# First net of a two-layer model: fourth and fifth chunk by seven block products, the half-wide chunk between them

## The chip, the core and the metric

The kernel runs on one core of a Trainium2 chip. The metric is the device time of one execution in microseconds (us), median of several runs. The five engines that matter are PE (TensorE, matrix products), DVE (VectorE), ACT (ScalarE), POOL (GpSimd) and SP (SyncE, which issues most DMA transfers). Each engine works its own queue of instructions in order; semaphores tie the queues together.

## The reference

Two layers, a sequence of 256 tokens, width 1024, everything in float32. A layer has two feed-forward nets (`ffn1`, `ffn2`) with a mixer and a cross attention between them. A net is

```python
def swiglu(x, w_gate, w_up, w_down):
    return (jax.nn.silu(x @ w_gate) * (x @ w_up)) @ w_down

h = layer_norm(ALPHA * h + 0.5 * swiglu(h, ffn1_gate[l], ffn1_up[l], ffn1_down[l]), ln_g[l, 0], ln_b[l, 0])
```

with `w_gate` and `w_up` of 1024 x 2816 and `w_down` of 2816 x 1024. The inner width of 2816 is five chunks of 512 columns and one of 256. The change touches only the first net of the first layer.

## The kernel before, in words

**Numbers in two parts.** A float32 matrix is split into a high part `hi` (rounded to the PE's own format, by ACT) and a low part `lo = x - hi` (by DVE); this is `split`, lines 61 and 62. A product is then three matmuls, hi x hi, hi x lo and lo x hi (`mm_rows`, through `product` at L105). Every weight that comes from HBM passes this way: a `raw` tile of 128 x 1024 lands by DMA (SP), ACT writes `whi`, DVE writes `wlo`, PE reads both. There are 6 `raw` buffers and 8 each of `whi` and `wlo`, so the splits can run at most 8 tiles ahead of PE.

**A chunk of a net** (`ffn`, L400 on) computes gate and up for 512 inner columns and all 256 tokens, then silu(gate) * up, then turns the result (`turn`: four DMAs `dealt`, DVE block transposes `square`, and a split into `ah` and `al`) so that it can be the stationary side of the down product. The down product of a chunk is two slabs, `both(c, 0)` and `both(c, 1)`, of 24 matmuls each, two weight tiles per slab, summed in four PSUM tiles `dn`. The slabs of a chunk are issued behind the gate and up products of later chunks, so that the turn is hidden. Three slabs, `end`, are held back to the layer norm (`finish`): there they are worked output half by output half (`tail`), 18 matmuls for each of the four `dn` tiles, so that the norm of the first tokens can begin while the rest is still being summed.

**Three ways to make a chunk.**
- `hidden`: 48 matmuls for gate and 48 for up; 8 weight tiles, each read for 12 matmuls; on DVE 8 splits and four multiplications `gated` (L440).
- `last_hidden`: the chunk of 256 columns, 64 matmuls (half of them of 256 columns), 4 weight tiles.
- `by_seven`: gate and up side by side are one 1024 x 1024 matrix, x is 256 x 1024; cut into 2 x 2 blocks, their product takes seven block products (Strassen's scheme in Winograd's form) in place of eight. A block product (`run`) is 12 matmuls. The sums of blocks of x (`bx`) are made once per net. The sums of weight blocks are made by DVE for each chunk: `parts_of` with `plus` adds two tiles of 128 x 1024 (L597), four times two additions. Each of the seven products then needs two tiles split, 14 in all, and each tile is read for 6 matmuls. The results are combined on DVE from PSUM by seven `put` (L619); `left` does the last three, then silu and two multiplications (L649), then `turn`. Four raw blocks are held at once: in `spare0` and `spare1`, in `lng` and `lnb` (the buffers of the norm's parameters, filled later by `ln_params`, L296 and L297), in two `raw`, and in `spare2` and one `raw`.

**The order of the first net before** (`early` is not None there): first, hidden(1), hidden(2), hidden(3), seven(4), half(5). From the third chunk on, chunk c is followed by slab 1 of chunk c-2 and slab 0 of chunk c-1. Beside hidden(1) and hidden(2), DVE also makes `bx`, turns the second input `mem` (`turned`, in `spare0` and `spare1`) and computes small parameters (L268 to L288, whose rows lie in `spare2`). The other three nets use `sevens = (2, 4)` and are not touched.

**Who orders what.** The instructions of an engine are put in a fixed order when the program is built; loads are issued ahead as buffers come free, and SP issues them strictly in order, so a load that waits for its buffer holds back all loads behind it.

Of the kernel before, what the change touches and what calls it, by code (L numbers as in the profile page):

```python
# [28 lines left out]
CHUNK = 512  # L29
# [17 lines left out]
def model(ctx: ExitStack, tc: tile.TileContext, t: dict, out: bass.AP):  # L47
# [12 lines left out]
    def split(hi, lo, src):  # L60
        nc.scalar.copy(hi, src)  # L61
        lows.append(nc.vector.tensor_tensor(lo, src, hi.bitcast(F32), op=ALU.subtract))  # L62

    def load(src, k0, nk, c0, ncol, fine=False):


        hi, lo, todo = [], [], []
        step = 2048 // ncol
        for a in range(k0, k0 + nk, step):
            half = step // 2  # L70
            raw = [
                wp.tile([P, 1024], F32, tag="raw", name="raw", bufs=6).rearrange("p (k c) -> p k c", c=ncol)
                for _ in range(2)
            ]
            part = 1 if fine else half
            for b in range(0, step, part):
                loads.append(nc.sync.dma_start(
                    raw[b // half][:, b % half : b % half + part, :],
                    src[(a + b) * P : (a + b + part) * P, c0 : c0 + ncol].rearrange("(k p) c -> p k c", p=P),
                ))  # L80
            for s in range(2):
                h = wp.tile([P, 1024], F32R, tag="whi", name="whi", bufs=8)
                w = wp.tile([P, 1024], F32R, tag="wlo", name="wlo", bufs=8)
                h = h.rearrange("p (k c) -> p k c", c=ncol)
                w = w.rearrange("p (k c) -> p k c", c=ncol)
                r = raw[s]
                if fine:
                    todo += [(h[:, b, :], w[:, b, :], r[:, b, :]) for b in range(half)]
                else:
                    split(h, w, r)  # L90
                hi.append(h)
                lo.append(w)
        return Weights(hi, lo, half, todo)
# [20 lines left out]
    def mm_cols(w, cols, x):  # L114
        o = acc()
        for k in range(NK - 1):
            product(o, w.at(k, cols)[0], x[:, k], k == 0, False)
        for k in range(NK):
            product(o[:, 0, :], w.at(k, cols)[1], x[:, k, 0, :], False, False)
        product(o, w.at(NK - 1, cols)[0], x[:, NK - 1], False, True)  # L120
        return sums(o)

    def add(dst, o):
        dst = dst if len(dst.shape) == 3 else halves(dst)
        nc.scalar.copy(dst, o[:, 1])
        nc.vector.tensor_tensor(dst, o[:, 0], dst, op=ALU.add)
# [273 lines left out]
    def ffn(l, name, n, pend=None, last=False, early=None):  # L400
        gate, up, down = (t[f"{name}_{x}"][l] for x in ("gate", "up", "down"))
        with tc.tile_pool(name="ffn", bufs=2, reuse_waits="tile") as fp:
            acts = []

            def act_tiles():
                ah = fp.tile([P, 4, SEQ], F32R, tag="ah", name="ah", bufs=3)
                al = fp.tile([P, 4, SEQ], F32R, tag="al", name="al", bufs=3)
                return ah, al
# [5 lines left out]
            def all_products(w):  # L414
                o = [acc((P, CHUNK)) for _ in range(NT)]
                for a in range(0, NK, 2):
                    for i in range(NT):
                        for k in range(a, a + 2):
                            products(o[i], w, i, k)
                return o  # L420

            def activations():
                return fp.tile([P, NT, CHUNK], F32, tag="sg", name="sg", bufs=1)
# [10 lines left out]
            def activate(s, i, og):  # L434
                for v, o in by_two(s[:, i, :], og):
                    nc.scalar.activation(v, o, AF.Silu)

            def gated(s, i, ou):
                for v, o in by_two(s[:, i, :], ou):
                    nc.vector.tensor_tensor(v, o, v, op=ALU.mult)  # L440
# [5 lines left out]
            def turn(s):  # L446
                ah, al = act_tiles()
                x = fp.tile([P, 4, NT, P], F32, tag="dealt", name="dealt", bufs=1)
                for a in range(4):
                    nc.sync.dma_start(x[a * 32 : a * 32 + 32], s[:, :, a * P : (a + 1) * P])  # L450
                for i in range(NT):
                    d = fp.tile([P, 4, P], F32, tag="up", name="square")
                    nc.vector.transpose(
                        d.rearrange("p k (b r) -> p b k r", b=4), x[:, :, i, :].rearrange("p b (k j) -> p b k j", k=4)
                    )
                    split(ah[:, :, tok(i)], al[:, :, tok(i)], d)
                return ah, al
# [80 lines left out]
            def hidden(c0, between=lambda: None):  # L538
                s = activations()
                o = all_products(load(gate, 0, NK, c0, CHUNK))  # L540
                for i in range(NT):
                    activate(s, i, o[i])
                between()
                o = all_products(load(up, 0, NK, c0, CHUNK))
                for i in range(NT):
                    gated(s, i, o[i])
                return turn(s)
# [106 lines left out]
            def last_hidden(c0):  # L654

                ah, al = act_tiles()
                s = activations()[:, 0, :].rearrange("p (j c) -> p j c", j=2)
                r = fp.tile([P, 2, SEQ], F32, tag="up", name="up")
                for m, o in ((gate, s), (up, r)):
                    w = load(m, 0, NK, c0, 2 * P)  # L660
                    for j in range(2):
                        add(o[:, j, :], mm_cols(w, slice(j * P, (j + 1) * P), xT))
                    if m is gate:
                        nc.scalar.activation(s, s, AF.Silu)
                nc.vector.tensor_tensor(s, r, s, op=ALU.mult)
                for j in range(2):
                    split(
                        *(x[:, j, :].rearrange("p (i b r) -> p i b r", i=2, b=4) for x in (ah, al)),
                        s[:, j, :].rearrange("p (i r b) -> p i b r", i=2, b=4),
                    )  # L670
                return ah, al

            def slab(c, u):
                w = load(down, c * 4 + 2 * u, 2, 0, DM)
                ah, al = acts[c]
                return w, ah[:, 2 * u : 2 * u + 2, :], al[:, 2 * u : 2 * u + 2, :]


            sevens = (2, 4) if early is None else (4,)
            bx = []  # L680

            if early is None:
# [5 lines left out]
            chunks = [(c, min(CHUNK, DFF - c)) for c in range(0, DFF, CHUNK)]  # L688
# [7 lines left out]
            def both(c, u):  # L696
                a = slab(c, u)
                for i in range(NT):
                    for k in range(2):
                        for m in range(2):  # L700
                            apart = last and i == m == k == u == 1 and c == 3
                            rows_of(a, i, k, m, c == u == k == 0, apart)
# [6 lines left out]
                    else:  # L709
                        bx.extend(blocks_of_x())  # L710

            for c, (c0, ncol) in enumerate(chunks):
                if not c:
                    acts.append(first())
                    ys = [[acc((P, 512), "dn") for _ in range(2)] for _ in range(NT)]
                elif c in sevens:
                    left = by_seven(c0, bx)
                else:
                    if c in (1, 2) and early is not None:
                        acts.append(hidden(c0, aside))  # L720
                    else:
                        acts.append(hidden(c0) if ncol == CHUNK else last_hidden(c0))
                if c == 1 and early is None:
                    bx.extend(blocks_of_x())
                if c == max(sevens) + 1:
                    gb = ln_params(l, n)
                if c == 1 and early is not None:

                    with tc.issue_after(loads[-1].ins):
                        rest = early(fp)  # L730
                if c == 2 and early is not None:
                    with tc.issue_after(lows[-1].ins):
                        rest[0]()
                if c > 0:
                    if c > 1:
                        both(c - 2, 1)
                    if c in sevens:
                        acts.append(left())
                    if c < len(chunks) - 1:
                        both(c - 1, 0)  # L740
            end = [slab(4, 0), slab(4, 1), slab(5, 0)]

            def tail(i, m, cols, alone, between):
                for u, a in enumerate(end):
# [476 lines left out]
```

## Time and profile before

| | |
|---|---|
| time, median of 3 runs (lowest to highest) | 1070.83 us (1070.54 to 1071.65) |
| span of the profiled execution | 1068.8 us |
| median less span | 2.0 us |
| ACT busy | 642.4 us (60%) |
| POOL busy | 66.4 us (6%) |
| HBM read | 216.15 MB |

The profile has busy time by engine, the chain of work that ended last, groups of instructions by line with their mean duration and the idle time ahead of them, and a timeline. Durations of neighbours overlap: an instruction of an engine starts a little before the one ahead of it is reported done, so the cost of one more instruction in a row is the distance between starts, not its duration. Matmuls overlap more strongly: one lasts 380 ns, but they start about 216 ns apart.

### The profile page before, as it was taken

The page shows a single profiled execution, that of the slowest core. Times are in us where ns is not written, and L with a number is a line of the kernel's source. Part 1 is how long each engine was busy: PE and PEld are TensorE (multiplying, and loading weights), DVE is VectorE, ACT ScalarE, POOL GpSimd, SP SyncE. Part 2 cuts the span into 40 slices and gives each one's busy share as a digit, 9 for nine tenths or more (in the row PEclk, how much of TensorE's full clock was granted, in tenths as well). Part 3 has the DMA queues.
Part 4 walks back from the last instruction along what each step waited for, and adds up shares of the span by engine and source line. Part 5 has one row for each costly group of instructions (what it writes and reads, how often), then busy time and mean ns, then how long its engine had stood idle before and what let it go on. Part 6 is the DMA issues. An engine that isn't in the chain of part 4 may idle for free.

```text
span 1068.8 us, 16312 instructions
## 1 busy us (share of the span) xinstructions
PE 1059.3 (99%) x5966; PEld 937.7 (88%) x5966; DVE 946.3 (89%) x1318; ACT 642.4 (60%) x916; POOL 66.4 (6%) x114
## 2 busy tenths in 40 slices
PE   9999999999999999999999999999999999999997
PEld 7888888889899888888888888888898998888886
DVE  6977997998988799999799999788989787999996
ACT  7555664666557565656575557566764665656660
POOL 9700001000000000000000000010000000000000
PEclk9999999999999999999999999999999999999999
DMA  9997484755574575848675865856536665759461
GB/s 362 262 307 256 129 288 165 249 176 174 170 278 167 178 252 194 290 167 218 238 272 184 256 254 183 290 179 216 196 126 213 241 227 181 257 156 334 134 223 40
DMA packets 130895, 231.90 MB, mean 217 GB/s; under 512 B 9408, under 2 KB 48608, under 8 KB 130816
## 3 DMA queue, kind: packets, MB, share of 16 engines
q1 hardware_dynamic: 129024, 228.49, 64.8%
q0 software_dynamic: 1216, 1.20, 0.5%
q8 instruction: 47, 0.77, 0.3%
q10 hardware_dynamic: 576, 1.18, 0.3%
q14 instruction: 32, 0.26, 0.1%
HBM read 216.15 MB, written 1.05 MB: 203 GB/s over the span
## 4 chain that ended last, share of the span: by engine, by line
PE 99%; DMA 0%; DVE 0%; issue 0%; DVEq 0%
PE acc L105 65%; PE dn L105 31%; PE acc L172 1%; PE dn L923 1%; PE dn L982 0%; DMA h<-in_x_dram 0%; PE acc L491 0%; PE dn L981 0%; PE dn L971 0%; PE acc L1047 0%; PE dn L888 0%; DVE h L358 0%; DVE h L353 0%; PE dn L472 0%; DVE st L338 0%
## 5 line engine op out<-in xcount | busy, mean ns | idle before, releaser
L61 ACT CAST whi<-raw 128x1024 fp32r<-128x1024 f32 (+1 forms) x438 | 442.9, 1042 | 197.5 <-DVE raw L597 54.9
L62 DVE TENSOR_TENSOR wlo<-raw,whi 128x1024 fp32r<-128x1024 f32 (+1 forms) x438 | 515.7, 1209 | 32.6 <-ACT whi L61 29.0
L105 PE MATMUL acc<-whi,xT 128*128 128x512 f32 x1032 | 312.9, 380 | 0.0
L105 PEld LDWEIGHTS acc<-whi,xT 128*128 128x128 f32 x1032 | 195.1, 189 | 27.5
L105 PE MATMUL acc<-wlo,xT 128*128 128x512 f32 x516 | 195.6, 379 | 0.0
L105 PE MATMUL acc<-xT,whi 128*128 128x512 f32 x576 | 142.3, 383 | 0.2
L105 PE MATMUL dn<-whi,ah 128*128 128x512 f32 x346 | 131.5, 380 | 0.0
L105 PE MATMUL dn<-wlo,ah 128*128 128x512 f32 x346 | 131.2, 379 | 0.0
L105 PE MATMUL dn<-whi,al 128*128 128x512 f32 x346 | 131.2, 379 | 0.0
L105 PEld LDWEIGHTS acc<-xT,whi 128*128 128x128 f32 x576 | 104.0, 190 | 12.5 <-ACT whi L61 0.7
L105 PEld LDWEIGHTS acc<-wlo,xT 128*128 128x128 f32 x516 | 97.5, 189 | 13.8
L105 PE MATMUL dn<-whi,xT 128*128 128x512 f32 x288 | 87.9, 381 | 0.0
L105 PEld LDWEIGHTS acc<-xT,wlo 128*128 128x128 f32 x576 | 75.5, 191 | 3.9
L105 PE MATMUL acc<-xT,wlo 128*128 128x256 f32 x576 | 75.9, 275 | 0.0
L105 PEld LDWEIGHTS dn<-whi,al 128*128 128x128 f32 x346 | 65.4, 189 | 9.2
L105 PEld LDWEIGHTS dn<-wlo,ah 128*128 128x128 f32 x346 | 65.4, 189 | 9.2
L105 PEld LDWEIGHTS dn<-whi,ah 128*128 128x128 f32 x346 | 65.4, 189 | 9.1
L350 POOL TENSOR_TENSOR rs<-rs,nhalf 128x1 f32<-128x1 f32 x16 | 14.9, 930 | 833.6 <-DVE rs L346 598.1
L597 DVE TENSOR_TENSOR raw<-raw 128x1024 f32<-128x1024 f32 x56 | 66.2, 1217 | 0.4
L105 PEld LDWEIGHTS dn<-whi,xT 128*128 128x128 f32 x288 | 54.4, 189 | 7.7 <-DVE xT L62 0.3
L105 PE MATMUL dn<-wlo,xT 128*128 128x512 f32 x144 | 54.6, 379 | 0.0
L332 DVE SCALAR_TENSOR_TENSOR h<-h,dn 128x512 f32<-128x512 f32 x31 | 21.2, 683 | 32.9 <-PE dn L105 32.9
(234 smaller groups left out, 1277.5 us busy)
## 6 DMA issues: line engine op xcount, KB each, us to landing
raw<-in_ffn_up_dram SPq DMA_DIRECT2D x88, 512.0 KB, 5.3
raw<-in_ffn_down_dram SPq DMA_DIRECT2D x88, 512.0 KB, 6.6
raw<-in_ffn_gate_dram SPq DMA_DIRECT2D x84, 512.0 KB, 5.1
raw<-in_w_in_dram SPq DMA_DIRECT2D x48, 512.0 KB, 4.7
dealt<-sg SPq DMA_DIRECT2D x80, 128.0 KB, 4.7
raw<-in_ca_k_dram SPq DMA_DIRECT2D x16, 512.0 KB, 4.9
raw<-in_w_out_dram SPq DMA_DIRECT2D x16, 512.0 KB, 4.5
raw<-in_ca_v_dram SPq DMA_DIRECT2D x16, 512.0 KB, 5.3
```

What stands on the lines that cost most here:

```text
L61: nc.scalar.copy(hi, src)
L62: lows.append(nc.vector.tensor_tensor(lo, src, hi.bitcast(F32), op=ALU.subtract))
L105: nc.tensor.matmul(o, w, x, start=start, stop=stop)
L172: nc.tensor.transpose(pt[:, k, :], src[:, (4 * j + k) * P : (4 * j + k + 1) * P], unit)
L332: nc.vector.scalar_tensor_tensor(v, v, ALPHA / scale, sums(y[i][n]), op0=ALU.mult, op1=ALU.add, accum_out=None if junk is None else st[:, ...
L350: nc.gpsimd.tensor_tensor(rs, rs, nhalf[:, 0:1], op=ALU.pow)
L597: nc.vector.tensor_tensor(r[i], r[i], plus[i], op=ALU.add)
L923: nc.tensor.matmul(o[g, hh, :], kc[:, hh, g], x, start=True, stop=True)
```

## The change

In the first net alone, `sevens` becomes `(3, 4)`, the order of chunks becomes 0, 1, 2, 3, 5, 4, and the slabs held back to the norm are slab 0 of the half-wide chunk 5 and both slabs of chunk 4. Behind seven(3) come `both(1, 1)` and `both(2, 0)`; behind half(5) only `both(2, 1)`; behind seven(4) `both(3, 0)`, the rest of chunk 4 (`left`) and `both(3, 1)`. `acts` becomes a dictionary, and `ln_params` is called in the last turn of the loop. The code for the other nets gives the same order as before.

```diff
-            sevens = (2, 4) if early is None else (4,)
+            sevens = (2, 4) if early is None else (3, 4)
...
-            for c, (c0, ncol) in enumerate(chunks):
+            acts = {}
+            order = [0, 1, 2, 3, 4, 5] if early is None else [0, 1, 2, 3, 5, 4]
+            for at, c in enumerate(order):
+                c0, ncol = chunks[c]
...
-                if c == max(sevens) + 1:
+                if at == 5:
                     gb = ln_params(l, n)
...
-                if c > 0:
-                    if c > 1:
-                        both(c - 2, 1)
+                if at == 5 and early is not None:
+                    both(3, 0)
+                    acts[c] = left()
+                    both(3, 1)
+                elif at > 0:
+                    if at > 1:
+                        both(order[at - 2], 1)
                     if c in sevens:
-                        acts.append(left())
-                    if c < len(chunks) - 1:
-                        both(c - 1, 0)
-            end = [slab(4, 0), slab(4, 1), slab(5, 0)]
+                        acts[c] = left()
+                    if at < 4 or early is None and at < 5:
+                        both(order[at - 1], 0)
+            end = [slab(4, 0), slab(4, 1), slab(5, 0)] if early is None else [slab(5, 0), slab(4, 0), slab(4, 1)]
```

In the built program of the changed kernel DVE's queue is the same as before up to the last split of `mem`; behind it stand, up to the last weight split of seven(4), 38 splits of 128 x 1024, 16 additions of weight tiles and 47 shorter instructions. PE's order in the first net is 84 matmuls (seven(3)), 48, 64 (half(5)), 24, 84 (seven(4)), and then 48 and 72 of the down product, with the 8 transposes of the norm's result among the last 9.

More of the change, by code (lines that the diff above doesn't have):

```diff
@@ L402, in ffn @@
         with tc.tile_pool(name="ffn", bufs=2, reuse_waits="tile") as fp:
-            acts = []
             def act_tiles():
@@ L710, in aside @@
                         bx.extend(blocks_of_x())
-            for c, (c0, ncol) in enumerate(chunks):
+            acts = {}
+            order = [0, 1, 2, 3, 4, 5] if early is None else [0, 1, 2, 3, 5, 4]
+            for at, c in enumerate(order):
+                c0, ncol = chunks[c]
                 if not c:
-                    acts.append(first())
+                    acts[c] = first()
                     ys = [[acc((P, 512), "dn") for _ in range(2)] for _ in range(NT)]
@@ L719, in ffn @@
                     if c in (1, 2) and early is not None:
-                        acts.append(hidden(c0, aside))
+                        acts[c] = hidden(c0, aside)
                     else:
-                        acts.append(hidden(c0) if ncol == CHUNK else last_hidden(c0))
+                        acts[c] = hidden(c0) if ncol == CHUNK else last_hidden(c0)
                 if c == 1 and early is None:
                     bx.extend(blocks_of_x())
-                if c == max(sevens) + 1:
+                if at == 5:
                     gb = ln_params(l, n)
```

## The prediction

> **What bounds the kernel now.** I read the page's busy times first, then the chain of work that ended last, then the timeline of DVE in the first net.
>
> ```profile
> PE 1059.3 (99%) x5966; PEld 937.7 (88%) x5966; DVE 946.3 (89%) x1318; ACT 642.4 (60%) x916; POOL 66.4 (6%) x114
> PEclk9999999999999999999999999999999999999999
> PE 99%; DMA 0%; DVE 0%; issue 0%; DVEq 0%
> ```
>
> PE is busy and on the chain for 99% of the span, at full granted clock in all slices; so a matmul less is time less, as long as nothing else comes late. DVE has 89% on average, and the stages differ. The chain in order of time gives PE's stretches in the first net (start, length, count):
>
> ```profile
> 75.27 10.36 PE dn L105 x48
> 85.63 20.72 PE acc L105 x96
> 106.35 10.36 PE dn L105 x48
> 116.71 18.13 PE acc L105 x84
> 134.84 10.36 PE dn L105 x48
> 145.20 10.48 PE acc L105 x64
> 155.68 18.13 PE dn L105 x84
> 173.81 0.87 PE acc L172 x8
> 177.28 7.86 PE acc L105 x48
> ```
>
> At 85.63 begins hidden(3), at 116.71 seven(4), at 145.20 half(5); at 177.28 the next stage begins. No gap lies between them. A matmul costs 20.72 / 96 = 0.216 us. The view by windows shows how much room DVE has over those stretches (PE busy, PEld, DVE, ACT, POOL, clock, DMA share, GB/s):
>
> ```profile
> 73.00:86.00 13.00, 13.00 (x63) 11.35 (x62) 8.66 (x11) 5.67 (x6) 0.00 (x0) 1.00 1.03 303
> 86.00:117.00 31.00, 31.00 (x146) 27.14 (x145) 28.34 (x43) 17.57 (x22) 0.00 (x0) 1.00 0.54 186
> 117.00:146.00 29.00, 29.00 (x136) 25.41 (x135) 28.58 (x32) 19.87 (x22) 0.00 (x0) 1.00 0.66 206
> 146.00:162.00 16.00, 16.00 (x92) 14.45 (x91) 14.30 (x19) 12.60 (x17) 0.00 (x0) 1.00 0.90 329
> ```
>
> In the 89 us DVE is idle for 4.3 + 2.7 + 0.4 + 1.7 = 9.1 us. This is the stage that the change loads.
>
> **The change part by part.** *PE gains 12 matmuls*: 96 become 84 in chunk 3, 12 x 0.216 = 2.59 us. The order of the rest costs PE nothing by itself: the same slabs, the same 72 matmuls at the end, the same 8 transposes.
>
> *DVE gains work.* Its prices are distances between starts in runs of neighbours:
>
> ```profile
> 69.73 1.30 DVE L202 STREAM_TRANSPOSE turned<-m 128x512 f32<-128x512 f32 x2
> 73.26 3.49 DVE L62 TENSOR_TENSOR wlo<-raw,whi 128x1024 fp32r<-128x1024 f32 x3
> 89.93 0.18 DVE L268 COPY prm<-acc 128x32 f32<-128x32 f32 x1
> 94.14 2.36 DVE L62 TENSOR_TENSOR wlo<-raw,whi 128x1024 fp32r<-128x1024 f32 x2
> 105.81 0.75 DVE L440 TENSOR_TENSOR sg<-acc,sg 128x256 f32<-128x256 f32 x2
> 106.47 1.22 DVE L62 TENSOR_TENSOR wlo<-raw,whi 128x1024 fp32r<-128x1024 f32 x1
> 109.40 3.49 DVE L597 TENSOR_TENSOR raw<-raw 128x1024 f32<-128x1024 f32 x3
> 112.81 2.35 DVE L62 TENSOR_TENSOR wlo<-raw,whi 128x1024 fp32r<-128x1024 f32 x2
> 117.35 1.30 DVE L453 STREAM_TRANSPOSE square<-dealt 128x512 f32<-128x512 f32 x2
> 118.57 1.19 DVE L62 TENSOR_TENSOR wlo<-raw,whi 128x1024 fp32r<-128x1024 f32 x1
> 119.67 1.28 DVE L62 TENSOR_TENSOR al<-square,ah 128x512 fp32r<-128x512 f32 x2
> 120.88 5.76 DVE L62 TENSOR_TENSOR wlo<-raw,whi 128x1024 fp32r<-128x1024 f32 x5
> 126.55 0.69 DVE L619 TENSOR_TENSOR half<-acc,sg 128x512 f32<-128x512 f32 x1
> 127.15 2.35 DVE L62 TENSOR_TENSOR wlo<-raw,whi 128x1024 fp32r<-128x1024 f32 x2
> 129.42 0.69 DVE L619 TENSOR_TENSOR sg<-acc,half 128x512 f32<-128x512 f32 x1
> 159.23 1.60 DVE L62 TENSOR_TENSOR al<-sg,ah 128x256 fp32r<-128x256 f32 x2
> 160.87 2.36 DVE L62 TENSOR_TENSOR wlo<-raw,whi 128x1024 fp32r<-128x1024 f32 x2
> ```
>
> A weight split: (126.55 - 120.88) / 5 = 1.135 us. An addition of weight tiles: (112.81 - 109.40) / 3 = 1.137. A `put`, or one of the multiplications after it: 127.15 - 126.55 = 0.60. A `gated`, or a sum of the half chunk: 0.66 / 2 = 0.33. A block transpose 0.61, an `al` split 0.605, one of the half chunk 1.64 / 2 = 0.82. The small parameters: 94.14 - 89.93, less two splits, 1.94 in all.
>
> A hidden chunk has 8 splits and 4 `gated`, 10.4 us; a seven has 14 splits, 8 additions, 7 `put` and 2 multiplications, 30.4 us. So DVE gets 20.0 us more, against 9.1 us in which it is idle over the whole stretch, while PE would be there 2.59 us sooner. That alone says that DVE comes late; how late follows from its queue.
>
> Up to 73.26 DVE's queue does not differ. From there the built program has, up to the 14th weight split of seven(3): 14 splits (15.89), 8 additions (9.10), 4 `gated` (1.32), the turn of chunk 2 (2 transposes and 2 `al`, 2.43), the small parameters (1.94) and 4 `put` (2.40), together 33.1 us: the split is done at 106.3. PE begins seven(3) at 85.63 and reads a tile for 6 matmuls, 1.295 us, so it wants the 14th tile 13 x 1.295 = 16.83 us later, at 102.46. It waits 3.9 us there. Most of it is one wait, at the start of the seventh product: that one also needs the PSUM tile that two `put` empty, and these stand behind the addition ahead of that last split.
>
> Then come 24 splits (the 4 tiles of `both(1, 1)` and `both(2, 0)`, 4 of half(5), 2 of `both(2, 1)`, 14 of seven(4); 27.24), 8 additions (9.10), 10 `put` and multiplications (6.00), 4 sums of the half chunk (1.32), chunk 3's turn (2.43) and the half chunk's `al` (1.64): 47.7 us. So the 14th split of seven(4) is done at 73.26 + 33.1 + 47.7 = 154.06. PE without a wait would begin seven(4) at 85.63 + 18.13 + 10.36 + 10.48 + 5.18 = 129.78 and want that tile at 146.61. It is 7.45 us late. The half chunk with its one slab is too short to pay the debt back.
>
> Before, the same tally ended well: the 14th split of seven(4) was done where the row of 129.42 begins, and PE wanted it at 116.71 + 16.83 = 133.54, 4.1 us later. DVE had made its additions ahead, beside hidden(3), whose eight tiles go slowly (2.59 us each). In the changed kernel no such chunk lies ahead of either seven.
>
> From 154.06, PE needs 1.29 us for the last 6 matmuls of seven(4), then 120 matmuls of the down product (25.91) and the transposes (0.87): the next stage begins at 182.1, in place of 177.28. That is **+4.85 us**, with the 2.59 us gained already in it.
>
> *The end of the net.* Chunk 4 is now made last, and the tail needs it 48 + 6 matmuls after its last product. The rows of one turn before, and of the silu that stands ahead of it:
>
> ```profile
> 134.85 0.63 ACT L648 ACTIVATE sg<-sg 128x512 f32<-128x512 f32 x1 [1.51 <-DVE sg L619]
> 139.79 0.69 DVE L649 TENSOR_TENSOR sg<-sg,half 128x512 f32<-128x512 f32 x1 [0.42 <-ACT sg L648]
> 140.51 2.70 SPq L450 DMA_DIRECT2D dealt<-sg  x4
> dealt<-sg SPq DMA_DIRECT2D x80, 128.0 KB, 4.7
> 149.04 1.21 ACT L61 CAST ah<-square 128x512 fp32r<-128x512 f32 x2 [0.75 <-DVE square L453]
> ```
>
> Behind 154.06 DVE has two splits, three `put`, a split and two multiplications, to 160.5. SP issues the four transfers until 163.2; the last lands 4.7 us after its issue, at about 167.4. DVE, which has six more splits to do, reaches the transposes at 167.3. One transpose (0.61), ACT's cast (0.60) and an `al` (0.6) later, at 169.2, chunk 4 can be read for the first tokens; PE is there at 155.35 + 11.65 = 167.0 and its third matmul wants `al` at 167.4. I take **+1.8 us**. The bounds are 0 and 3: a quicker landing gives at most 0.2 back, since the six splits stand there anyway; the slab of the half chunk, 1.3 us, is the only work between.
>
> *Waits of DVE that the tally leaves out.* Its own idle time before in this stretch, whose releasers the groups by line name:
>
> ```profile
> L62 DVE TENSOR_TENSOR wlo<-raw,whi 128x1024 fp32r<-128x1024 f32 x48 | 57.1, 1218 | 4.9 <-ACT whi L61 4.6
> L453 DVE STREAM_TRANSPOSE square<-dealt 128x512 f32<-128x512 f32 x6 | 3.9, 688 | 3.6 <-DMA dealt<-sg 3.6
> ```
>
> Those 8.5 us came while DVE was ahead, with no free buffer or nothing landed. With a debt it should not run into full buffers, so I take 0.5 us, for the second tile of seven(3): its load waits until `turned` has read `spare1` (the row of 69.73, so 71.0); if it lands 4.7 us later, as `dealt` does, ACT has cast it at 76.8, near where DVE's queue wants it. The bounds are 0 and 8.5.
>
> *SP's queue.* The loads of seven(4) into `lng` and `lnb` stand behind chunk 2's `dealt` and ahead of half(5)'s; they wait for the 7th and 8th split of seven(3) (92 and 95), and behind them wait the half chunk's loads, first split by DVE at about 115. 20 us is ample beside a landing of about 5 us, so I cost it at nothing; if the cover went, DVE would idle and each us would be a us. ACT has 60% and is not late.
>
> The sum is 4.85 + 1.8 + 0.5 = **+7.1 us**. The span of 1068.8 becomes 1075.9; the median stands 2.0 above the span, so 1070.83 becomes **1077.9 us**.
>
> [...] A weight split is reported with 1218 ns, and five in a row take 5.76 us. [...]
>
> **The rivals.**
> 1. *PE stays the bound, and it is faster.* If DVE kept pace, as beside seven(4) before (18.13 us for 84 matmuls, no gap), only the tail could wait: -2.59 + 1.8 = -0.8, at best -2.6: 1068.2 to 1070.0 us. It decides at 16.83 us after a seven's start: all 14 splits must be done by then. Against it stand the 20.0 us of work against 9.1 us of room.
> 2. *DVE idles on top.* Chunk 3's blocks come while DMA is full (share 1.03 in the first window), and DVE's queue holds additions that wait for landings with everything behind them. If it idles by 3 to 7 us, the time is 1080.5 to 1085 us.
> 3. *The debt is smaller*, by work that I priced too high or a PE order that forgives: 0 to +4.5 us, 1070.8 to 1075.3.
> [...]
>
> **How the numbers follow.** Forecast, DVE late by 4.5 to 9.5 us net (1075.3 to 1080.3): 0.67. Rival 2: 0.13. Rival 3: 0.10, of which a third within 0.2%. Rival 1: 0.06. Rival 4: 0.04. A measurement of this kernel can tell about 0.2% (2.1 us) from no change; rival 1 reaches that only at its best end. Faster by more: 0.04; within: 0.06; slower: 0.90. The range 1074 to 1083 leaves out rival 1, most of rival 3 and a third of rival 2, about 0.2.
>
> **What would show it.** Right: stretches of PE in seven(3) and seven(4) longer than 18.13 us, about 22 each, with waits released by DVE's `wlo` or `put`; DVE 97% or more busy from 74 to 160; a wait of 1 to 3 us of PE in the tail, on `ah` or `al` of chunk 4; the next stage beginning near 184. Wrong: both sevens at 18.13 us, or DVE idle for more than 3 us there, or a granted clock below 1 in that stretch.

## The result, and the profile after

The changed kernel takes **1078.27 us** (median of 5 runs, 1077.13 to 1080.63) against 1070.83 before: ratio 1.0071, 95% interval 1.006 to 1.0081, slower by 7.4 us. The profiled execution took 1078.07 us, with a span of 1076.3.

The page of the changed kernel: busy times, then the granted clock by slices, then the shares of the chain by engine.

```profile
span 1076.3 us, 16310 instructions
PE 1061.4 (99%) x5954; PEld 935.9 (87%) x5954; DVE 964.8 (90%) x1337; ACT 647.5 (60%) x921; POOL 66.5 (6%) x114
PEclk9999999999999999999999999999999999999999
PE 82%; DVE 9%; DMA 4%; issue 2%; ACT 2%; SPq 1%; DVEq 0%; ACTq 0%
```

On the average over the span hardly anything has moved: PE still shows 99%. What tells is the chain: PE carried 99% of it, now 82%. The rest runs over DVE, over casts on ACT and over landings, that of chunk 4's `dealt` among them. So there is a stretch in which PE isn't the bound. The view by windows of the changed kernel finds it (columns as in the prediction):

```profile
86.00:117.00 31.00, 28.23 (x126) 23.15 (x125) 30.86 (x48) 22.48 (x26) 0.00 (x0) 1.00 0.61 189
117.00:146.00 29.00, 26.64 (x138) 23.16 (x137) 28.42 (x32) 16.96 (x23) 0.00 (x0) 1.00 0.50 161
74.00:160.00 86.00, 80.87 (x376) 68.71 (x375) 85.22 (x107) 54.06 (x64) 0.00 (x0) 0.98 0.58 183
```

In the last row DVE has no room left: 85.22 of 86 us, 99%. PE, busy in all of the same 86 us before, is idle for 5.1 of them by its reported durations, which overlap. The timeline of PE shows where; these are the first matmuls of the stretches and the longest waits (in brackets the idle time and its releaser):

```profile
85.50 0.38 PE L105 MATMUL acc<-whi,xT 128*128 128x512 f32 x1
105.29 0.48 PE L105 MATMUL acc<-whi,xT 128*128 128x512 f32 x1 [0.73 <-ACT whi L61]
106.55 0.48 PE L105 MATMUL acc<-wlo,xT 128*128 128x512 f32 x1 [0.78 <-DVE wlo L62]
107.74 0.38 PE L105 MATMUL dn<-whi,ah 128*128 128x512 f32 x1
133.76 0.38 PE L105 MATMUL acc<-whi,xT 128*128 128x512 f32 x1
143.50 0.48 PE L105 MATMUL acc<-whi,kTh 128*128 128x512 f32 x1 [0.52 <-ACT whi L61]
145.83 0.50 PE L105 MATMUL acc<-wlo,kTh 128*128 128x512 f32 x1 [1.84 <-DVE wlo L62]
156.47 0.38 PE L105 MATMUL dn<-whi,ah 128*128 128x512 f32 x1
171.05 0.48 PE L105 MATMUL dn<-whi,ah 128*128 128x512 f32 x1 [0.18 <-ACT ah L61]
184.14 1.67 PE L105 MATMUL acc<-mT,whi 128*128 128x512 f32 x7
```

Seven(3) lasts from 85.50 to 107.74, 22.2 us; seven(4) from 133.76 to 156.47, 22.7. Without a wait each would be 18.1, so 8.7 us are lost in them, against the 2.6 us that twelve matmuls less save. The next stage begins at 184.14. In the kernel before, the same first matmul stands at

```profile
177.11 1.67 PE L105 MATMUL acc<-mT,whi 128*128 128x512 f32 x7
```

so 7.03 of the 7.5 us by which the span grew are lost in the first net.

### The profile page after: what moved, and what is told of

Same layout as the page of the kernel before. It is cut to its first block, busy times and chain, and to the rows that moved or that the text cites. A ratio compares the mean times of both kernels' runs of the same rounds, so it can differ in the third digit from the quotient of the medians.

```text
span 1076.3 us, 16310 instructions
## 1 busy us (share of the span) xinstructions
PE 1061.4 (99%) x5954; PEld 935.9 (87%) x5954; DVE 964.8 (90%) x1337; ACT 647.5 (60%) x921; POOL 66.5 (6%) x114
## 4 chain that ended last, share of the span: by engine, by line
PE 82%; DVE 9%; DMA 4%; issue 2%; ACT 2%; SPq 1%; DVEq 0%; ACTq 0%
PE acc L105 54%; PE dn L105 25%; DVE wlo L62 4%; DMA dealt<-sg 2%; DMA raw<-in_ffn_gate_dram 1%; DVE raw L595 1%; PE acc L172 1%; ACT whi L61 1%; DMA raw<-in_ffn_up_dram 1%; SPq L448 1%; PE dn L928 1%; DVE half L617 0%; DVE al L62 0%; DVE square L451 0%; DVE sg L438 0%
## 5 line engine op out<-in xcount | busy, mean ns | idle before, releaser
L61 ACT CAST whi<-raw 128x1024 fp32r<-128x1024 f32 (+1 forms) x444 | 447.4, 1041 | 207.0 <-DVE raw L595 70.8
L62 DVE TENSOR_TENSOR wlo<-raw,whi 128x1024 fp32r<-128x1024 f32 (+1 forms) x444 | 522.0, 1208 | 31.0 <-ACT whi L61 27.9
L105 PE MATMUL acc<-whi,xT 128*128 128x512 f32 x992 | 301.6, 380 | 1.6 <-ACT whi L61 0.7
L105 PEld LDWEIGHTS acc<-whi,xT 128*128 128x128 f32 x992 | 187.5, 189 | 29.1 <-issue 1.6
L105 PE MATMUL acc<-wlo,xT 128*128 128x512 f32 x496 | 188.1, 379 | 0.8 <-DVE wlo L62 0.8
L105 PEld LDWEIGHTS acc<-wlo,xT 128*128 128x128 f32 x496 | 93.7, 189 | 14.3 <-DVE wlo L62 1.1
L595 DVE TENSOR_TENSOR raw<-raw 128x1024 f32<-128x1024 f32 x64 | 75.5, 1215 | 0.4
L105 PE MATMUL acc<-wlo,kTh 128*128 128x512 f32 x128 | 49.3, 385 | 1.8 <-DVE wlo L62 1.8
```

The source lines that it names most:

```text
L105: nc.tensor.matmul(o, w, x, start=start, stop=stop)
L595: nc.vector.tensor_tensor(r[i], r[i], plus[i], op=ALU.add)
```

## The experiments

All times are medians, and the kernel before had 1070.6 to 1071.1 us beside them. "Next stage" is the start of that first `acc<-mT,whi` matmul: 177.11 before, 184.14 in the changed kernel. The theory, D: DVE's queue owes the time, because a seven gives it 20 us more work and the stretch had 9.1 us of room.

**e1: the order alone.** The changed kernel with one seven:

```diff
-            sevens = (2, 4) if early is None else (3, 4)
+            sevens = (2, 4) if early is None else (4,)
```

> The new order of chunks and of the slabs held back, but chunk 3 made by 96 matmuls as before; only chunk 4 by seven. Theory D (DVE's queue cannot prepare two sevens): the DVE tally ends the 14th split of seven(4) near 134, PE wants it near 149, so no wait in seven(4); only the tail may wait for chunk 4's turn, 0 to 0.5 us: 1070.8 to 1071.3 us, 18.13 us for seven(4). Rival O (the order is at fault: chunk 4 last, its loads and its turn come late): most of the 7.4 us stays, 1076 to 1078 us.

Measured: 1074.22 us (1072.35 to 1076.03), ratio 1.0037 (1.0024 to 1.0049). Both theories missed. The sevens' part of it held: seven(4) takes 18.1 us and nothing waits in it. But the order alone isn't free. From the timeline of PE in this kernel:

```profile
166.84 0.48 PE L105 MATMUL dn<-whi,ah 128*128 128x512 f32 x1 [2.50 <-ACT ah L61]
180.66 1.67 PE L105 MATMUL acc<-mT,whi 128*128 128x512 f32 x7
```

At the tail PE waits 2.5 us for chunk 4's `ah`, and the next stage is 3.5 us late, with as many matmuls in this net as before. In the changed kernel the same wait is 0.2 us. Two things make the difference. PE's timeline has 63 matmuls between seven(4) and this wait in e1 and 66 in the changed kernel, so 0.65 us less cover (the prediction had counted 54). And `ah` comes later: PE reads it 16.3 us behind the end of seven(4) here (150.58 to 166.84), and 14.6 us there (156.47 to 171.05). The chain of each run has the last transfer of the turn, first in e1, then in the changed kernel:

```profile
158.60 6.51 DMA dealt<-sg
```

```profile
164.86 4.02 DMA dealt<-sg
```

It lands 6.5 us behind its issue in e1 and 4.0 in the changed kernel, whose other steps take 0.8 us longer; why isn't shown. The number of matmuls doesn't decide alone: e4, e9 and e10, below, have about 60 there and wait 0.2 to 0.6 us.

**e2: two sevens in the old order** (the kernel before with `sevens` (3, 4), the half chunk last).

> Chunks 3 and 4 by seven in the order of before, the half-wide chunk last, the slabs held back as before. Theory D: without the half-wide chunk between them DVE has 10 us less work but PE wants seven(4) 15.7 us sooner; by the tally the 14th split of seven(4) is done at 144.7 and wanted at 130.95, so about 13.7 us late, less 2.6 saved: +11, 1081 to 1083 us, nothing lost at the tail. Rival O (the order is at fault): 1068 to 1071 us.

Measured: 1087.7 us (1086.48 to 1089.53), ratio 1.0162 (1.0148 to 1.0175). D had the direction, and 5 us too little; O fell. Here only one slab of 10.4 us lies between the sevens, where the changed kernel has 26.0, and the debt is collected in ten waits in and around seven(4), the largest of them:

```profile
132.08 0.48 PE L105 MATMUL acc<-whi,kTh 128*128 128x512 f32 x1 [2.07 <-ACT whi L61]
```

Nothing waits at the tail. The next stage is 16.2 us late (193.52 against 177.28 in the chain). So with two sevens the half chunk between them helps by over 9 us, and it doesn't suffice. What made the loss 5 us larger than D's isn't worked out; in this run DVE was idle for 1.5 us from 136 to 140, and the granted clock was 0.72 from 132 to 138, with matmuls 0.43 us apart from 135.00 to 137.56.

**e3: the first of the sevens alone** (the kernel before with `sevens` (3,), and the loads of the norm's parameters left at chunk 5).

> Order of before; chunk 3 by seven in place of chunk 4, so one seven as before and the same matmul count as before. Theory D: DVE comes to seven(3) with no additions made ahead and is 4 to 5 us late at its last product; the hidden chunk behind it keeps that debt from growing: +4 to +5 us, 1074.8 to 1076 us. Rival S (only the second seven is too much; one seven at either place fits): 1070.8 us.

Measured: 1075.76 us (1075.06 to 1076.69), ratio 1.0049 (1.0036 to 1.0061): D. The timeline of PE, first matmul behind seven(3) and next stage:

```profile
108.86 0.38 PE L105 MATMUL dn<-whi,ah 128*128 128x512 f32 x1
182.37 1.67 PE L105 MATMUL acc<-mT,whi 128*128 128x512 f32 x7
```

From 85.99, seven(3) takes 22.9 us; all waits of this net stand in it. With the same number of sevens as before, it is slower by 5 us: a seven behind chunk 2 finds no stretch in which DVE can work ahead, the one behind hidden(3) does.

**e4: no additions.** The changed kernel without the sixteen additions of weight tiles in the first net's sevens; the sums of weight blocks aren't formed there.

```diff
-                        if plus is not None:
+                        if plus is not None and early is None:
                             nc.vector.tensor_tensor(r[i], r[i], plus[i], op=ALU.add)
```

> The changed kernel without the 16 additions of weight tiles in the first net (the sums of weight blocks are not formed; splits, loads, products and puts stay). Theory D: DVE's queue is 18.2 us shorter, the 14th splits are done near 97 and 136 and wanted at 102 and 147, so the waits go: the 2.59 us come out, less 0 to 1 us at the tail: 1068.2 to 1069.5 us. Rival O (loads, SP's queue, the late turn): it stays at 1075 to 1078 us.

Measured: 1069.42 us (1068.63 to 1071.31), ratio 0.9989 (0.998 to 0.9998): D. Each seven takes 18.1 us with no wait, and the next stage begins at 176.89:

```profile
176.89 1.67 PE L105 MATMUL acc<-mT,whi 128*128 128x512 f32 x7
```

In this execution 1.8 us of that are lost at the start of the program, where the same matmuls take longer (the granted clock is 1.00 in both, so the reason stays open); the chains of e4 and of the kernel before:

```profile
6.18 0.85 PE acc L489 x4
```

```profile
6.02 0.44 PE acc L491 x4
```

Seven(3) so begins at 87.33 in place of 85.50. Without that the next stage would begin at 175.06 (an estimate, which moves all of PE's work by those 1.83 us), which makes the sixteen additions worth 184.14 - 175.06 = 9.1 us; by the medians it is 8.9. This is also about the ceiling: with DVE 18 us lighter, the change brings 0.1% (0.02 to 0.2%).

**e9, e10: one seven's additions left out.** Does each seven pay for its own, or is there one debt? The addition stands under a condition on the chunk; the sums of that one seven aren't formed:

```diff
-                            nc.vector.tensor_tensor(r[i], r[i], plus[i], op=ALU.add)
+                            if early is None or c0 != 3 * CHUNK:     # e10: 4 * CHUNK
+                                nc.vector.tensor_tensor(r[i], r[i], plus[i], op=ALU.add)
```

> The changed kernel without the eight additions of weight tiles in the first net's seven for chunk 3 (left out: the sums of weight blocks there; the products read the blocks unsummed); seven for chunk 4 is whole. Theory D (one queue with one debt, which is carried from seven to seven: VectorE is 8 x 1.137 = 9.1 us sooner from chunk 3 on): the 14th split of seven(3) is done at about 97, before it is wanted, and that of seven(4) at about 154.9 - 9.1 = 145.8, 0.8 before PE wants it (146.6); both sevens run without more than 1 us of wait, and the time is 1069 to 1071 us: eight additions less are worth nearly as much as sixteen (1069.4). Rival E (each seven waits for its own additions): seven(4) still ends late by what it waits in the changed kernel, half of the 8.9 us between the changed kernel and the one without additions stay, and the time is 1073 to 1075 us.

> The changed kernel without the eight additions of weight tiles in the first net's seven for chunk 4 (left out: the sums of weight blocks there); seven for chunk 3 is whole. Theory D (one queue, one debt): seven(3) waits as in the changed kernel and takes 23.3 us in place of hidden(3)'s 20.72, and seven(4)'s 14th split is done at 145.8 where PE, now late, wants it at about 151.7: no wait there; so +2.6 us, and 0.4 at the end of the net: 1073 to 1074.5 us. Rival E (each seven waits for its own additions): the same half of 8.9 us stays as without chunk 3's, 1073 to 1075 us in both runs; the two theories part in the other run of this pair, and here in the wait in seven(4): none by D and E. Rival N (VectorE only idles instead, so that leaving out work late in the queue gives nothing): 1076 to 1078 us.

Measured: e9 1072.71 us (1071.34 to 1074.16), ratio 1.0015 (1.0006 to 1.0024); e10 1074.44 us (1072.32 to 1076.64), ratio 1.0033 (1.0023 to 1.0042). By its time e9 falls between the theories, so the timeline of PE has to tell. In e9:

```profile
147.17 0.48 PE L105 MATMUL acc<-whi,xT 128*128 128x512 f32 x1 [0.54 <-ACT whi L61]
148.43 0.48 PE L105 MATMUL acc<-wlo,xT 128*128 128x512 f32 x1 [0.78 <-DVE wlo L62]
177.21 1.67 PE L105 MATMUL acc<-mT,whi 128*128 128x512 f32 x7
434.01 0.48 PE L105 MATMUL acc<-wlo,xT 128*128 128x512 f32 x1 [0.78 <-DVE wlo L62]
```

Seven(3) doesn't wait. Seven(4), whose additions are all there, waits 1.9 us in place of 4.6: over half of its wait had come from the first seven, where E has all of it stay and D at most 1 us. The next stage begins at 177.21. Half the additions took 6.9 of the 7.0 us away in this net; E would have left about half. The other 1.5 us of e9's span, 1070.3, come mostly from a wait at 434.01 in the next net, whose code is the same. DVE's split there begins 1.5 us later than in the kernel before (432.73 and 431.27); what made that stays open. In e10 seven(3) lasts from 85.96 to 108.88, as e3's did, and seven(4), behind it, 18.1 us:

```profile
134.90 0.38 PE L105 MATMUL acc<-whi,xT 128*128 128x512 f32 x1
153.03 0.38 PE L105 MATMUL dn<-whi,ah 128*128 128x512 f32 x1
180.34 1.67 PE L105 MATMUL acc<-mT,whi 128*128 128x512 f32 x7
```

Additions left out early are worth more (6.9 us in this net) than as many left out late (3.8): so behaves one queue with one debt, in which work out of the first seven pays for the second as well. By the medians, 5.6 and 3.8 us below the changed kernel, the gap is smaller. The 3.8 in this net is rather too small: in this execution DVE's first additions begin at 75.89, in the changed kernel at 74.74, though the code up to there is the same, so up to 1.1 us of e10's loss come from elsewhere. Whether both together are worth less than their sum isn't shown: 9.1 against 10.7 by the timelines, but 8.9 against 9.4 by the medians.

**e5, e6, e7: the additions on GpSimd.** The addition's `nc.vector` becomes `nc.gpsimd`: e5 in the first net of the changed kernel, e6 in the first net of e2's, e7 in all seven sevens of the kernel before (56 additions).

> The changed kernel, with the sixteen additions of weight tiles in the first net's two sevens made on GpSimd in place of VectorE; nothing is left out. Theory D (VectorE's queue is the debt, 9.1 us of it the sixteen additions' half per seven): 18.2 us of VectorE work go, as in the run without additions, so both sevens take 18 to 19 us, and the time is 1068.5 to 1070.5 us, if one addition on GpSimd takes below about 2.5 us (no row here shows it; the nearest is its memset of 128 x 1024 with 0.95 us). Rival P (the additions only change place: what counts is that a product needs a sum, and GpSimd is slower or holds VectorE up while it works): VectorE's weight splits show more than 1.135 us from start to start beside GpSimd's additions, and the time is 1074 to 1080 us.

> The kernel before with sevens for chunks 3 and 4 of the first net, in the old order (half chunk last), and their sixteen additions on GpSimd. Theory D: no weight addition is left on VectorE in the first net, and the turn of chunk 4 has the half chunk and its slabs behind it, so nothing waits at the end of the net: PE keeps its 2.59 us, less about 1 us at the starts of the products; 1068.2 to 1070 us, below the kernel before (1070.6) by 0.1 to 0.2%. Rival P (GpSimd slow or in VectorE's way): the wait in seven(4) stays, as in the old order with the additions on VectorE (1087.7 us), 1076 to 1088 us.

> The kernel before, only with the weight additions of all its sevens made on GpSimd. It tells what GpSimd's additions do where VectorE is not late. Theory D: nothing waits for VectorE there, so the time stays within 0.2% of before, 1069 to 1072.5 us. Rival P (GpSimd slow or in VectorE's way): products of the sevens wait for sums, and with eight and more sevens in the program the time rises by 5 us or more, to 1076 us or above.

Measured: e5 1096.52 us (ratio 1.0237, 1.0223 to 1.0251), e6 1097.83 (1.0252, 1.0238 to 1.0266), e7 1115.13 (1.0414, 1.0399 to 1.0428). Rival P, in e5 and e6 further than it said. Two timelines of e5, GpSimd's and DVE's, tell why:

```profile
76.14 17.08 POOL L595 TENSOR_TENSOR raw<-raw 128x1024 f32<-128x1024 f32 x6 [25.13 <-DVE wlo L62]
143.19 2.38 POOL L595 TENSOR_TENSOR raw<-raw 128x1024 f32<-128x1024 f32 x1 [1.16 <-DVE wlo L62]
146.73 2.36 POOL L595 TENSOR_TENSOR raw<-raw 128x1024 f32<-128x1024 f32 x1 [1.16 <-DVE wlo L62]
```

```profile
79.52 0.74 DVE L438 TENSOR_TENSOR sg<-acc,sg 128x256 f32<-128x256 f32 x2
143.37 3.28 DVE L62 TENSOR_TENSOR wlo<-raw,whi 128x1024 fp32r<-128x1024 f32 x1
146.91 3.27 DVE L62 TENSOR_TENSOR wlo<-raw,whi 128x1024 fp32r<-128x1024 f32 x1
```

The addition that begins at 143.19 ends at 145.57. DVE's split that begins at 143.37 ends at 146.65, 1.08 us behind that: as if it stood still until GpSimd was done and then took its own time. The second pair is the same (149.09, 150.18). So an addition on GpSimd costs DVE about 2.1 us there (3.28 less 1.2) where its own took 1.14. Not all of DVE's work stands still: `gated`, with one input in PSUM, takes its usual 0.37 each at 79.52, in the midst of six additions that run on GpSimd from 76.14 to 93.22.

In these rows the split, with two inputs in SBUF, took 3.28 us in place of 1.2. Two operations didn't grow: `gated` (0.37) and the block transposes of 95.47, with one input, 1.30 us for two as in the kernel before, beside two additions on GpSimd (94.38 to 101.08):

```profile
94.38 6.70 POOL L595 TENSOR_TENSOR raw<-raw 128x1024 f32<-128x1024 f32 x2 [1.16 <-DVE wlo L62]
95.47 1.30 DVE L451 STREAM_TRANSPOSE square<-dealt 128x512 f32<-128x512 f32 x2
```

So these runs don't take the debt away, they nearly double the price of what makes it, which fits D; D's expectation for them failed on the premise that GpSimd takes work off DVE. Behind the longer waits PE's granted clock was down as well (0.50 from 102 to 106 in e5, below), and products wait for sums that GpSimd makes; how the 18 us that e5 loses against the changed kernel divide among these isn't shown.

**e8: PE kept busy in the gap.** Nine matmuls whose result isn't used stand ahead of the matmul of 143.50.

```diff
                     for k in range(4):
+                        if k == 2 and warm is not None:
+                            for n in range(9):
+                                nc.tensor.matmul(warm, bx[0][0][:, 0, :], bx[0][0].rearrange("p k t -> p (k t)"), start=True, stop=True)
```

> The changed kernel with nine more matmuls (128x512, their results unused) at the place in the fourth chunk's neighbour, chunk 4's seven, where PE waits 0.5 and 1.8 us for a sum of weight blocks and then runs at a granted clock of 0.5 to 0.6 for 3.5 us. Theory D: the clock stays near 1.0 in 146 to 150 us, since no idle stretch over 1.5 us is left; but the end of that seven hangs on VectorE's 14th weight split (about 154.9 us), so the next stage begins at most 0.5 us sooner and the time is 1077.5 to 1078.5 us. Rival C (the fallen clock is what the debt at the fourth chunk's neighbour costs, 1.75 us): the next stage begins 1.7 us sooner, and the time is 1076.3 to 1076.8 us.

Here are the windows of PE behind the wait (busy, clock, DMA share, GB/s), first of the changed kernel, then of e8, and three rows of e8's timeline:

```profile
146.00:148.00 2.00, 2.00 (x6) 0.54 0.43 164
148.00:150.00 2.00, 2.00 (x8) 0.61 0.87 190
```

```profile
146.00:148.00 2.00, 1.85 (x9) 1.00 0.42 106
148.00:150.00 2.00, 1.99 (x10) 1.00 0.70 217
```

```profile
155.35 0.48 PE L105 MATMUL acc<-wlo,xT 128*128 128x512 f32 x1 [0.77 <-DVE wlo L62]
156.54 0.38 PE L105 MATMUL dn<-whi,ah 128*128 128x512 f32 x1
184.43 1.67 PE L105 MATMUL acc<-mT,whi 128*128 128x512 f32 x7
```

The clock stays at 1.00 and nothing is gained: PE now comes to the last tile of seven(4) early and waits there for DVE's 14th split (the row of 155.35), seven(4) ends at 156.54 in place of 156.47, and the next stage begins 0.29 us later than in the changed kernel. About 0.27 of that was there in seven(3) already. Rival C fell; the fallen clock lay beside DVE's debt. The median of four runs is 1080.57 us (1078.45 to 1083.26, ratio 1.0093), above both expectations; the profiled one, of 1078.45, has nothing that would explain the 2.1 us above it, so that stays open.

## Why the prediction was right, step by step

*PE gains 12 matmuls, 2.59 us.* So it is: e4, without the debt, has 18.1 us where hidden(3) had 20.7.

*DVE gains 20 us against 9.1 us of room; the tally.* It was the right account, and its prices held: three splits in a row from 105.27 to the next operation at 108.69 are 1.14 us apart. The 14th split of seven(3) was put at 106.3, that of seven(4) at 154.06. DVE's timeline in the changed kernel (the first of the three, and the second of the four, are these splits):

```profile
105.27 3.50 DVE L62 TENSOR_TENSOR wlo<-raw,whi 128x1024 fp32r<-128x1024 f32 x3
108.69 0.68 DVE L617 TENSOR_TENSOR half<-acc,half 128x512 f32<-128x512 f32 x1
152.63 4.61 DVE L62 TENSOR_TENSOR wlo<-raw,whi 128x1024 fp32r<-128x1024 f32 x4
168.50 1.23 DVE L62 TENSOR_TENSOR wlo<-raw,whi 128x1024 fp32r<-128x1024 f32 x1 [1.44 <-ACT whi L61]
169.65 1.30 DVE L451 STREAM_TRANSPOSE square<-dealt 128x512 f32<-128x512 f32 x2
```

They are done at 106.4 and, 2.27 us from 152.63, at 154.9. Behind the second PE was expected at the down product at 155.35 and came at 156.47. But it didn't wait for that split, as the working had it: its wait in seven(4) was at 145.83, earlier, and behind it PE ran at about half the clock (0.54 and 0.61) until 149.5 and reached the last tile 0.3 us after the split. The wait at the 14th split that the prediction had is seen in e8, where the clock stays up, with the same end. In seven(3) the prediction had most of the lateness in one wait, at the seventh product; that was wrong in shape: it comes in small ones of 0.4 to 0.8 us. The end is as it was put (107.6 by the working, 107.74 measured).

*DVE's own waits, 0.5 us.* In the stretch it idled for 0.8 (86 less 85.22), though not at the start of seven(3), for which the term stood: the listed waits are 0.4 us for a cast at 120.30 and 0.2 at 136.22. Together, the part ahead of the tail is: down product at 156.47, 26.78 us to go without a wait, less 177.11, so +6.14; the terms gave 4.85 + 0.5 = 5.35. **Too small by 0.8**: the 14th split came 0.3 later than the terms put it, PE needed 0.3 more behind it, and 0.17 is the prediction's own start, which it read off the chain (177.28) and not off the timeline (177.11).

*The tail, 1.8 us.* Between 156.47 and 184.14 lie 27.67 us, so 0.9 us of waits, 0.2 of it listed for chunk 4's `ah`. **Too large by 0.9**, though every step of DVE came later than it was put (transposes at 169.65, not at 167.3). The wrong part was the sentence that the slab of the half chunk, counted with 6 matmuls ahead of the wait, is the only work between: PE's timeline has 66 matmuls there, so 18 of that slab, 2.6 us more cover. The last transfer landed in 4.0 us, where 4.7 stood; in e1, with 6.5 us for it and 63 matmuls of cover, the wait is 2.5 us. The order in which a program is built has to be counted, not read off the loop.

So the two mis-sized terms cancel to 0.1. Behind this net another 0.5 us come, and 1.8 in place of 2.0 lie around the span: 1068.8 + 7.03 + 0.47 + 1.77 = 1078.07 for the profiled execution, where 1077.9 stood. The mechanism was right, that DVE's queue falls behind and PE waits for it, and the closeness of the number is in part luck.

*SP's queue at nothing.* No row of PE's or DVE's waits names a landing in the two sevens; the weight tiles came in time. Rival 2, DVE idle on top, so didn't come. Rival 1, no debt, is what e4 shows when the additions are gone, and with 1069.42 inside that rival's 1068.2 to 1070.0. Rival 3, a smaller debt, is what e9 shows, with half of them gone. For the change as it stands both are out, with 1078.27.

*Rival 4, the clock.* The granted clock fell, at another place than where it would count: to 0.54 and 0.61 from 146 to 150, behind the wait of seven(4), and not at the tail, where it stood at 1.00 in every window from 156 to 184. e8, with 1.00 from 146 to 150, shows that it cost nothing there. The prediction named a granted clock below 1 in the stretch as a sign of being wrong; it was no such sign. The view by slices, 27 us wide, doesn't show it, the windows of 2 us do.

## What to carry over

Where two engines both stand near 100% in a stretch, a trade of 2.6 us of the one for 20 us of the other is judged by that stretch's idle time, not by the average of 89%. A queue's debt is carried from stage to stage: work taken out early in it paid more here than as much taken out late (5.6 and 3.8 us by the medians, 6.9 and 3.8 in the net), and once the debt is gone PE sets the time (18.1 us for a seven in e4). Before moving vector work to GpSimd, look at what DVE reads meanwhile: beside its operations with two inputs in SBUF the move gave nothing back here (e5 took 1096.52 us, the changed kernel 1078.27).

## What the runs showed of the hardware

GpSimd's addition of two 128 x 1024 tiles took 2.36 us alone and 2.85 in a row of six (17.08 us), and DVE's operations with two inputs in SBUF took up to 3.28 us in place of 1.2 meanwhile (e5, above).

The granted clock fell behind a gap with work in it. In the changed kernel PE ran out at 142.83 (one spacing behind its last start), made one matmul at 143.50, and went on at 145.83, 3.0 us later: 0.54 and 0.61 in the next two windows, matmuls 0.42 us apart in place of 0.216. In e5 a gap of 2.8 us, also with one matmul in it (91.57 to 94.35), left the clock at 1.00; behind one of 5.6 us, ahead of the matmul of 102.47, it was 0.50, and so it was behind one of only 2.7 us without a matmul in it (151.63 to 154.34; the view by windows of e5, with the clock as the third number from the end):

```profile
92.03 0.48 PE L105 MATMUL acc<-whi,kTh 128*128 128x512 f32 x1 [0.30 <-ACT whi L61]
94.35 0.48 PE L105 MATMUL acc<-wlo,kTh 128*128 128x512 f32 x1 [1.84 <-DVE wlo L62]
102.47 0.77 PE L105 MATMUL acc<-whi,kTh 128*128 128x512 f32 x1 [5.48 <-DVE prm L268]
151.41 0.39 PE L105 MATMUL acc<-whi,kTh 128*128 128x512 f32 x1
154.34 0.79 PE L105 MATMUL acc<-wlo,kTh 128*128 128x512 f32 x1 [2.54 <-DVE wlo L62]
```

```profile
104.00:106.00 2.00, 2.00 (x6) 1.57 (x5) 2.00 (x5) 1.81 (x3) 0.00 (x0) 0.50 0.46 83
154.00:156.00 2.00, 1.66 (x4) 1.39 (x5) 2.00 (x3) 2.00 (x3) 1.63 (x1) 0.50 0.00 0
```

So the clock fell once behind 3.0 us with a matmul inside and once behind 2.7 us without one, and not behind 2.8 us with one inside: the length of a gap alone doesn't decide it in these traces.
